# A hybrid mLSTM / gated DeltaNet layer: GpSimd's long two-operand operations cut into pieces of 256 columns

## The chip, the core and the metric

One core of one Trainium2 chip runs the whole layer. The metric is the device time in microseconds (us) of one execution. The engines are named as the profile names them: PE is the matrix engine (PEld is its weight load), DVE the vector engine, ACT the scalar engine, POOL is GpSimd, SP issues the DMAs.

## What is computed

The layer normalises x (2048 tokens of 1024 features, fp32), projects it with one matrix `w_in`, and feeds the columns to two groups of heads: four mLSTM heads (q and k of 128, v of 256) and eight gated DeltaNet heads (128 each, with a short causal convolution on q, k and v). Both are recurrences over chunks of tokens. Their gated and normalised outputs stand side by side (2048 columns), are projected with `w_out`, added to x, and normalised again. The core of the reference, cut:

```python
def step(carry, inp):                  # mLSTM, chunk by chunk
    ...
    P = jnp.exp(D - m_t[..., None]) * jnp.einsum('bhld,bhsd->bhls', qi, ki)
    num = (w_inter[..., None] * jnp.einsum('bhld,bhde->bhle', qi, C)
           + jnp.einsum('bhls,bhse->bhle', P, vi))
    ...
# gated DeltaNet, chunk by chunk: a unit lower triangular system, then a state update
sol = lax.linalg.triangular_solve(a_mat, rhs, left_side=True, lower=True, unit_diagonal=True)
U, W = sol[..., :dv], sol[..., dv:]
def step(S, inp):
    qi, ki, Ui, Wi, Ai, gi = inp
    v_new = Ui - jnp.einsum('bhld,bhde->bhle', Wi, S)
    o = (jnp.einsum('bhld,bhde->bhle', qi * jnp.exp(gi)[..., None], S)
         + jnp.einsum('bhls,bhse->bhle', Ai, v_new))
    ...
```

## The kernel before

**Layout.** The tokens are done in 4 segments of 512, each of 4 chunks of 128. A segment runs 8 windows in turn, P0 M0 P1 M1 P2 M2 P3 M3: P windows are pairs of DeltaNet heads, M windows mLSTM heads (the last segment has P3 before M2). In a window PE multiplies the segment's normalised input with the window's columns of `w_in`, and between these matmuls the chunk work of earlier windows is woven in. After the last segment comes the tail: 16 tiles of 128 tokens, each transposed and multiplied with `w_out`.

**Products in two parts.** Every fp32 product of the projections is made of three matmuls on parts: each operand is split into a high part (a cast, `hi`) and a low part (the operand less its high part, `lo`), and hi·hi, hi·lo and lo·hi are added in one PSUM tile. So each split needs a cast on ACT and a subtraction with two SBUF operands on DVE or POOL. Input parts are `hh` and `hl`, weight parts `whi` and `wlo`.

**Weights.** In segment 0 `split_w` loads a raw half (`wraw`, 128 x 1024), ACT casts it in two pieces of 512 columns (L175), and one subtraction makes the low part (L177): on DVE for the first four weights, on POOL for the 58 halves after them. Both parts are also written to DRAM (L181), and segments 1 to 3 load them from there (L157) with no splitting. The names ending in _P belong to P windows, those in _M to M windows. PE reads a weight half as four steps k of 256 columns: L343 to L345 for the projections that keep features on the partitions (`pf_...`), L355 to L357 for those that keep tokens there (`pt_...`); L345 and L356 are the ones that read `wlo`.

**Other two-operand work of POOL.** `load_h` scales the next segment's input by the row norm (`rbc`, L316) and the gain (`attn_c`, L319), 8 halves of 512 columns a segment, for segments 1 to 3. Once per DeltaNet head q (`gq`) is multiplied by its decay `gbc` (L845), 512 columns; the mLSTM multiplies `qw` by `qT` (L541) and splits it (L553). In the tail POOL applies the gain to the transposed tile (`ytt`, L1188) and makes its low part (`ylo`, L1153), four groups of 512 columns for each token tile.

**Work around it on DVE.** The solver of the triangular blocks is 31 pairs of a product `tb` (L816) and a subtraction `xb` (L820), both on SBUF alone. Others read one operand from PSUM (`gyt`, L985: the gate on the product `op`), or move 32 x 32 blocks (stream transposes: L484, and L1185 for the tail).

**Order.** PE's order is the order of the code. That of the other engines' queues is set when the kernel is built, by a scheduler that simulates the instructions; each engine then runs its own queue strictly in turn and waits on semaphores. A semaphore wait covers the part of a tile that was written, not the whole tile: who reads one piece waits for the instruction that wrote this piece.

Of the kernel before, what the change touches and what calls it, by code (L numbers as in the profile page):

```python
# [10 lines left out]
F32 = mybir.dt.float32  # L11
F32R = mybir.dt.float32r
AF = mybir.ActivationFunctionType
ALU = mybir.AluOpType
# [3 lines left out]
P = 128  # L18
D = 1024
KT = D // P  # L20
T = 512
# [24 lines left out]
RAW = 'hkhrhrkkkrrry'  # L46
WOM = 2
WFP = 100
GN = 4


VT = ((0, 1, 1, 1), (1, 1, 1, 1), (1, 0, 0, 0))
# [13 lines left out]
def hybrid_layer(  # L66
# [16 lines left out]
    nc = tc.nc  # L83
# [34 lines left out]
    attn_c = cst.tile([P, KT], F32, name="attn_c")  # L118
# [29 lines left out]
    def unit(ncol, dt, nm):  # L148
        return wp.tile([P, HK, ncol], dt, tag="wu", name=nm, bufs=10)
# [11 lines left out]
    def split_w(key, src, ncol, nm, between):  # L161

        raws = [unit(ncol, F32, f"wraw_{nm}_{i}") for i in range(2)]
        step = 2 if between else HK
        for k in range(0, KT, step):
            nc.sync.dma_start(raws[k // HK][:, k % HK:k % HK + step, :], src[:, k:k + step, :])
            if between:
                between()
        his, los = ([unit(ncol, F32R, f"{p_}_{nm}_{i}") for i in range(2)] for p_ in ("whi", "wlo"))
        eng = nc.vector if len(wloads) > nloads - WDV else nc.gpsimd  # L170
        for k in range(0, KT, step):
            i, k0 = k // HK, k % HK
            hi, lo, raw_ = his[i], los[i], raws[i]
            for q in range(k0, k0 + step, 2):
                nc.scalar.copy(hi[:, q:q + 2, :], raw_[:, q:q + 2, :])  # L175
            ks = slice(k0, k0 + step)
            eng.tensor_tensor(lo[:, ks, :], raw_[:, ks, :], hi[:, ks, :].bitcast(F32), op=ALU.subtract)  # L177
        kept = parts_d[key] = ypool.tile([2, 2, P, HK, ncol], F32, tag=f"wd{nm}", name=f"wd{nm}")
        for i in range(2):
            for part, t_ in enumerate((his[i], los[i])):  # L180
                nc.sync.dma_start(kept[part, i], t_.bitcast(F32))  # L181
        return his, los
# [121 lines left out]
    def load_h(seg, rbc):  # L304
        xks = []
        for t in range(NCH):
            if t == 2:
                ab = [sm.tile([P, 4, P], F32, tag="xin", name=f"xk{seg}_{t}_{i}") for i in range(2)]
            else:
                pool, tag, bufs = (wkp, "lbt", 1) if t == 3 else (sm, "xk", XKB)  # L310
                xk = pool.tile([P, KT, P], F32, tag=tag, name=f"xk{seg}_{t}", bufs=bufs)
                ab = [xk[:, 0:4, :], xk[:, 4:8, :]]
            c0 = seg * T + t * P
            for i in range(2):
                nc.sync.dma_start(ab[i], xT[:, i * 4:(i + 1) * 4, c0:c0 + P])
                nc.gpsimd.tensor_tensor(  # L316
                    ab[i], ab[i], rbc[:, t * P:(t + 1) * P].unsqueeze(1).broadcast_to([P, 4, P]),
                    op=ALU.mult)
                nc.gpsimd.tensor_tensor(  # L319
                    ab[i], ab[i], attn_c[:, i * 4:(i + 1) * 4].unsqueeze(2).broadcast_to([P, 4, P]),  # L320
                    op=ALU.mult)
            xks.append(ab)
        return xks

# [151 lines left out]
    def by_dve(which, seg, pr):  # L476
        return which[2 if seg == NSEG - 1 else min(seg, 1)][pr]
# [49 lines left out]
    def m_chunks(seg, h, r, st):  # L527
        s_ = f"{seg}_{h}"
        qT, kT, vt, G = r["q"], r["k"], r["v"], r["g"]
# [8 lines left out]
                pt[:, cs], nm[:, cs], ccol[:, c, h:h + 1], negmask, op0=ALU.add, op1=ALU.min)  # L538
            nc.scalar.activation(nm[:, cs], nm[:, cs], AF.Exp, bias=mprev[:, c, h:h + 1])
        qw = nm  # L540
        nc.gpsimd.tensor_tensor(qw, qw, qT, op=ALU.mult)  # L541
        nc.scalar.activation(pt, pt, AF.Exp)
        kq = psc.tile([P, 512], F32, tag="cp", name=f"kq{s_}")
        for c in range(NCH):
# [4 lines left out]
        if fast:  # L549
            def split(a, nm, pool, tag, eng, **kw):  # L550
                t_ = pool.tile([P, 2, T], F32R, tag=tag, name=f"{nm}{s_}", **kw)
                nc.scalar.copy(t_[:, 0, :], a)
                eng.tensor_tensor(t_[:, 1, :], a, t_[:, 0, :].bitcast(F32), op=ALU.subtract)  # L553
                return t_
            ps2 = split(pt, "pts", wkp, "lbt", nc.vector)
            qw2 = split(qw, "qws", sm, "xk", nc.gpsimd, bufs=XKB)
# [146 lines left out]
    def g_prep(seg, pr, r, st):  # L703
        s_ = f"{seg}_{pr}"
        h0 = pr * 2
        qT, kT = [r["q", 0], r["q", 1]], [r["k", 0], r["k", 1]]
# [3 lines left out]
        ua, gbcs = [uat[:, 0], uat[:, 1]], []  # L710
# [103 lines left out]
        for i in range(31):  # L814
            n = 31 - i
# [14 lines left out]
        for j in range(2):  # L830
            tp = psc.tile([P, 512], F32, tag="cp", name=f"qtp{s_}_{j}")
            if by_dve(QT, seg, pr):
                nc.scalar.activation(tp, qT[j], AF.Square)
                nc.vector.tensor_reduce(qs[:, j], tp.rearrange("p (b i) -> p b i", i=32),
                                        axis=mybir.AxisListType.X, op=ALU.add,
                                        apply_transpose=True)
            else:
                for c in range(NCH):
                    nc.tensor.transpose(tp[:, c * P:(c + 1) * P], qT[j][:, c * P:(c + 1) * P], ident)
                for c in range(NCH):  # L840
                    cs = slice(c * P, (c + 1) * P)
                    nc.scalar.activation(tp[:, cs], tp[:, cs], AF.Square,
                                         accum_out=ssq[:, c, j:j + 1])
            nc.scalar.activation(gbcs[j], gbcs[j], AF.Exp)
            nc.gpsimd.tensor_tensor(qT[j], qT[j], gbcs[j], op=ALU.mult)  # L845
            yield
        if by_dve(QT, seg, pr):

# [219 lines left out]
    for seg in range(NSEG):  # L1068
# [17 lines left out]
        for kind, n in ORDER_LAST if last else ORDER:  # L1086
            r = {}
            streams, keep = [], ()
            if kind == "P":
                q = 3 if n == 0 else n - 1  # L1090
# [54 lines left out]
    def gains(k, n):  # L1145
        return gain_c[:, k:k + n].unsqueeze(2).broadcast_to([P, n, P])

    def y_split(t, k4, yt_, eng, res):

        yh = fa.tile([P, 4, P], F32R, tag=f"yh{k4}", name=f"yh{t}_{k4}")  # L1150
        ylo = fa.tile([P, 4, P], F32R, tag=f"ylo{k4}", name=f"ylo{t}_{k4}")
        nc.scalar.copy(yh, yt_)  # L1152
        eng.tensor_tensor(ylo, yt_, yh.bitcast(F32), op=ALU.subtract)  # L1153
        res[k4] = yh, ylo

    def y_pe(t, yl, res):
# [18 lines left out]
    def y_dve(t, yl):  # L1175

        yts, n = [], 16 // len(yl)
        for k in range(0, 16, n):
# [4 lines left out]
            for a in range(4):  # L1183
                for b in range(4):
                    nc.vector.transpose(ytt[32 * b:32 * b + 32, :, 32 * a:32 * a + 32],  # L1185
                                        y3[32 * a:32 * a + 32, :, 32 * b:32 * b + 32])
            for c in range(0, n, GN):
                nc.gpsimd.tensor_tensor(ytt[:, c:c + GN, :], ytt[:, c:c + GN, :],  # L1188
                                        gains(k + c, GN), op=ALU.mult)
            yts += [ytt[:, c:c + 4, :] for c in range(0, n, 4)]  # L1190
# [78 lines left out]
    def raw_rows(k):  # L1269
        c = RAW[k - 3]  # L1270
        if c == "h":
            return raw_halves(k)
        if c == "k":
            return [sm.tile([P, D], F32, tag="xk", name=f"wor{k}", bufs=XKB)]
        if c == "r":
            return [fa.tile([P, D], F32, tag="xr", name=f"wor{k}", bufs=2)]
        return [fc.tile([P, D], F32, tag="yl", name=f"wor{k}", bufs=2)]

    for k in range(3, 16):
# [3 lines left out]
        raw_ = raw_rows(k)  # L1283
# [86 lines left out]
```

## Time and profile before

| | |
|---|---|
| three runs | 2354.9, 2358.06, 2360.65 us; median 2358.06 |
| the profiled execution | 2354.22 us; its span (first to last instruction) is 2352.2 us |
| mean granted TensorE clock in it | 0.976 of full speed |
| PE busy | 2225.8 us (95%) |
| DVE busy | 1925.3 us (82%) |
| ACT busy | 876.1 us (37%) |
| POOL busy | 714.5 us (30%), 820 instructions |

Busy time is the time in which an engine executes an instruction. An instruction of DVE or POOL that is held out of SBUF by another engine counts as busy for as long as it is held, so a busy engine is not always a working one: the same operation at two different durations is the sign to look for.

### The profile page before, as it was taken

To read this page: it belongs to the slowest core of one execution; us is meant where nothing else is said; L and a number is where in the kernel's file an instruction comes from. 1 tells how busy PE (TensorE), PEld (TensorE's weight loads), DVE (VectorE), ACT (ScalarE), POOL (GpSimd) and SP (SyncE) were. 2 spreads that over 40 slices of the span, in tenths; PEclk is the share of its full clock that TensorE was granted. 3 is DMA by queue.
4 is the path that set the end of the run, shared out by engine and by line. 5 is a ranking of instruction groups with operands and counts; after the bars stand their busy time and mean duration, and the time that the engine had idled before them with its cause. 6 is when DMAs were issued, how large, how long until landed. Compare 5 with 4: busy or idle time off the path is not lost.

```text
span 2352.2 us, 41574 instructions
## 1 busy us (share of the span) xinstructions
PE 2225.8 (95%) x14750; PEld 1970.7 (84%) x14750; DVE 1925.3 (82%) x5359; ACT 876.1 (37%) x2351; POOL 714.5 (30%) x820
## 2 busy tenths in 40 slices
PE   8889899889899999998999999999999999999998
PEld 7778788788789898887898989888988997777777
DVE  7989898996988888879888888788766837988784
ACT  5535454544333434343333343443334234111111
POOL 4435353451302121413020214130212114444433
PEclk9889999999999999999999999999999999999999
DMA  7766657574445554645454556454546455222221
GB/s 254 249 204 233 233 188 245 184 267 156 163 155 182 171 194 168 223 155 174 155 182 158 191 176 232 146 182 157 183 169 205 166 194 159 73 99 90 99 81 63
DMA packets 183320, 409.18 MB, mean 174 GB/s; under 512 B 51736, under 2 KB 84632, under 8 KB 183112
## 3 DMA queue, kind: packets, MB, share of 16 engines
q1 hardware_dynamic: 182392, 405.74, 50.9%
q8 instruction: 116, 1.90, 0.3%
q14 instruction: 92, 0.75, 0.1%
q10 hardware_dynamic: 720, 0.79, 0.1%
HBM read 309.68 MB, written 96.90 MB: 173 GB/s over the span
## 4 chain that ended last, share of the span: by engine, by line
PE 45%; DVE 37%; DMA 6%; issue 5%; ACT 3%; POOL 3%; SPq 0%; POOLq 0%; ACTq 0%; DVEq 0%
DVE ytt L1185 6%; DVE ktok L484 3%; DVE tb L816 3%; DVE xb L820 3%; DVE gv L484 2%; DVE kw L484 2%; PE pt_mz L355 2%; PE pt_mz L356 2%; PE pt_mz L357 2%; PE pt_mo L355 2%; PE pt_mo L356 2%; PE pt_mo L357 2%; PE pt_gz L356 2%; PE pt_gz L355 2%; PE pt_gz L357 2%
## 5 line engine op out<-in xcount | busy, mean ns | idle before, releaser
L1185 DVE STREAM_TRANSPOSE ytt<-yl 32x256 f32<-32x256 f32 x448 | 195.1, 436 | 42.0 <-POOL ylo L1153 35.9
L816 DVE TENSOR_TENSOR tb<-xb,lbt 128x248 f32<-128x248 f32 (+30 forms) x496 | 181.2, 365 | 20.5 <-DMA lbt<-l_d 7.7
L820 DVE TENSOR_TENSOR xb<-xb,tb 128x248 f32<-128x248 f32 (+30 forms) x496 | 172.0, 347 | 12.7
L983 POOL TENSOR_TENSOR gms<-gms,nhalf 128x2 f32<-128x2 f32 x64 | 46.8, 730 | 421.9 <-DVE gms L981 421.5
L355 PE MATMUL pt_mv<-whi_M,hh 128*128 128x256 f32 x512 | 149.3, 292 | 12.4 <-DVE vlo L511 8.3
L355 PE MATMUL pt_gz<-whi_P,hh 128*128 128x256 f32 (+1 forms) x512 | 153.8, 300 | 2.8 <-ACT whi_P L175 1.7
L355 PE MATMUL pt_mz<-whi_M,hh 128*128 128x256 f32 x512 | 150.1, 293 | 5.6 <-DVE tz L522 4.8
L355 PE MATMUL pt_mo<-whi_M,hh 128*128 128x256 f32 x512 | 149.4, 292 | 4.3 <-DVE vlo L511 4.3
L357 PE MATMUL pt_gz<-whi_P,hl 128*128 128x256 f32 (+1 forms) x512 | 148.3, 290 | 1.5 <-DVE mr L630 1.5
L356 PE MATMUL pt_gz<-wlo_P,hh 128*128 128x256 f32 (+1 forms) x512 | 148.4, 290 | 1.4 <-DVE wlo_P L177 1.4
L356 PE MATMUL pt_mv<-wlo_M,hh 128*128 128x256 f32 x512 | 145.9, 285 | 0.0
L357 PE MATMUL pt_mv<-whi_M,hl 128*128 128x256 f32 x512 | 145.8, 285 | 0.0
L357 PE MATMUL pt_mz<-whi_M,hl 128*128 128x256 f32 x512 | 145.8, 285 | 0.0
L356 PE MATMUL pt_mz<-wlo_M,hh 128*128 128x256 f32 x512 | 145.8, 285 | 0.0
L357 PE MATMUL pt_mo<-whi_M,hl 128*128 128x256 f32 x512 | 144.7, 283 | 0.0
L356 PE MATMUL pt_mo<-wlo_M,hh 128*128 128x256 f32 x512 | 144.6, 282 | 0.0
L1233 ACT ACTIVATE jkf<-xr 128x512 f32<-128x512 f32 (+1 forms) x33 | 20.5, 620 | 278.5 <-DVE xr L1231 144.9
L484 DVE STREAM_TRANSPOSE ktok<-gk 32x128 f32<-32x128 f32 x384 | 116.1, 302 | 5.4
L484 DVE STREAM_TRANSPOSE gv<-xingv 32x128 f32<-32x128 f32 x384 | 116.0, 302 | 5.4
L1226 PE MATMUL po<-woh,ylo 128*128 128x512 f32 (+1 forms) x297 | 115.1, 388 | 0.6 <-POOL ylo L1153 0.6
L1224 PE MATMUL po<-woh,yh 128*128 128x512 f32 (+1 forms) x297 | 114.5, 386 | 0.9 <-ACT yh L1152 0.9
L1225 PE MATMUL po<-wol,yh 128*128 128x512 f32 (+1 forms) x297 | 114.7, 386 | 0.2 <-POOL wol L1032 0.2
(403 smaller groups left out, 7535.9 us busy)
## 6 DMA issues: line engine op xcount, KB each, us to landing
whi_M<-wdM SPq DMA_DIRECT2D x96, 512.0 KB, 3.9
wlo_M<-wdM SPq DMA_DIRECT2D x96, 512.0 KB, 5.3
whi_P<-wdP SPq DMA_DIRECT2D x90, 512.0 KB, 3.8
wlo_P<-wdP SPq DMA_DIRECT2D x90, 512.0 KB, 5.0
wraw_M<-in_wg_dram SPq DMA_DIRECT2D x32, 512.0 KB, 6.8
wdM<-whi_M SPq DMA_DIRECT2D x32, 512.0 KB, 3.0
wdM<-wlo_M SPq DMA_DIRECT2D x32, 512.0 KB, 5.7
wraw_P<-in_wg_dram SPq DMA_DIRECT2D x30, 512.0 KB, 6.0
```

The costliest lines, as they stand in the source:

```text
L355: nc.tensor.matmul(ps, lhsT=hh[k][:, ts], rhs=hi, start=(k == 0), stop=False)
L356: nc.tensor.matmul(ps, lhsT=hh[k][:, ts], rhs=lo, start=False, stop=False)
L357: nc.tensor.matmul(ps, lhsT=hl[k][:, ts], rhs=hi, start=False, stop=(k == KT - 1))
L484: nc.vector.transpose(dst[32 * a:32 * a + 32, :, 32 * b:32 * b + 32], s4[32 * b:32 * b + 32, :, a, :])
L816: nc.vector.tensor_tensor(tb[:, :, 0:n], xb[:, :, i:i + 1].broadcast_to([P, 8, n]), lbt[:, i:i + 1, i + 1:32].broadcast_to([P, 8, n]), op= ...
L820: nc.vector.tensor_tensor(xs, xs, tb[:, :, 0:n], op=ALU.subtract)
L983: nc.gpsimd.tensor_tensor(ms, ms, nhalf[:, 0:2], op=ALU.pow)
L1185: nc.vector.transpose(ytt[32 * b:32 * b + 32, :, 32 * a:32 * a + 32], y3[32 * a:32 * a + 32, :, 32 * b:32 * b + 32])
L1224: nc.tensor.matmul(ps, lhsT=yh, rhs=woh, start=(k == 0), stop=False)
L1225: nc.tensor.matmul(ps, lhsT=yh, rhs=wol, start=False, stop=False)
L1226: nc.tensor.matmul(ps, lhsT=ylo, rhs=woh, start=False, stop=(k == 15))
L1233: nc.scalar.activation(jk[:, 0:n], xr[:, cs], AF.Square, accum_out=ssf[:, i:i + 1])
```

## The change

POOL's subtractions and products with two operands of 512 or 1024 columns are issued as several instructions of 256 columns each, over the same data in the same tiles. The work per element is the same, and so are the variants of the same lines that run on DVE. POOL's instructions go from 820 to 1146.

```diff
-GN = 4
+GN = 2
...
-            eng.tensor_tensor(lo[:, ks, :], raw_[:, ks, :], hi[:, ks, :].bitcast(F32), op=ALU.subtract)
+            for ks in [ks] if eng is nc.vector else [slice(q, q + 1) for q in range(k0, k0 + step)]:
+                eng.tensor_tensor(
+                    lo[:, ks, :], raw_[:, ks, :], hi[:, ks, :].bitcast(F32), op=ALU.subtract)
...
-                nc.gpsimd.tensor_tensor(
-                    ab[i], ab[i], rbc[:, t * P:(t + 1) * P].unsqueeze(1).broadcast_to([P, 4, P]),
-                    op=ALU.mult)
-                nc.gpsimd.tensor_tensor(
-                    ab[i], ab[i], attn_c[:, i * 4:(i + 1) * 4].unsqueeze(2).broadcast_to([P, 4, P]),
-                    op=ALU.mult)
+                for k in range(0, 4, 2):
+                    a_ = ab[i][:, k:k + 2]
+                    nc.gpsimd.tensor_tensor(
+                        a_, a_, rbc[:, t * P:(t + 1) * P].unsqueeze(1).broadcast_to([P, 2, P]),
+                        op=ALU.mult)
+                    nc.gpsimd.tensor_tensor(
+                        a_, a_, attn_c[:, i * 4 + k:i * 4 + k + 2].unsqueeze(2).broadcast_to([P, 2, P]),
+                        op=ALU.mult)
...
-        nc.gpsimd.tensor_tensor(qw, qw, qT, op=ALU.mult)
+        for hs in (slice(0, T // 2), slice(T // 2, T)):
+            nc.gpsimd.tensor_tensor(qw[:, hs], qw[:, hs], qT[:, hs], op=ALU.mult)
...
-                eng.tensor_tensor(t_[:, 1, :], a, t_[:, 0, :].bitcast(F32), op=ALU.subtract)
+                n = T if eng is nc.vector else T // 2
+                for i in range(0, T, n):
+                    hs = slice(i, i + n)
+                    eng.tensor_tensor(
+                        t_[:, 1, hs], a[:, hs], t_[:, 0, hs].bitcast(F32), op=ALU.subtract)
...
-            nc.gpsimd.tensor_tensor(qT[j], qT[j], gbcs[j], op=ALU.mult)
+            for hs in (slice(0, T // 2), slice(T // 2, T)):
+                nc.gpsimd.tensor_tensor(qT[j][:, hs], qT[j][:, hs], gbcs[j][:, hs], op=ALU.mult)
...
-        eng.tensor_tensor(ylo, yt_, yh.bitcast(F32), op=ALU.subtract)
+        for ks in [slice(0, 4)] if eng is nc.vector else [slice(0, 2), slice(2, 4)]:
+            eng.tensor_tensor(ylo[:, ks], yt_[:, ks], yh[:, ks].bitcast(F32), op=ALU.subtract)
```

`GN` is the number of 128-column blocks that one gain operation of L1188 takes. Cut are, on POOL: L177 (58 operations, each now four), and in two pieces each L316 and L319 (24 each), L541 (16), L553 (10), L845 (32), L1153 (60) and L1188 (60).

The first place is POOL's queue early in segment 0, at the first weight whose low part POOL makes (`wlo_P_0_2`, the DeltaNet pair 0, third weight, in two halves); `halo` and `xingq` are the convolution's borders. Before:

```order
L177 TENSOR_TENSOR wlo_P_0_2_0_565<-wraw_P_0_2_0_559,whi_P_0_2_0_563 128x1024 [waits DMAHW1_49,DMAHW7_49,PE_49,Activation_49]
L663 COPY halo<-xingq_0_0_605 128x3 [waits Activation_49,Pool_49]
L661 COPY xingq_0_1_642<-halo 128x3 [waits DVE_49]
L177 TENSOR_TENSOR wlo_P_0_2_1_566<-wraw_P_0_2_1_560,whi_P_0_2_1_564 128x1024 [waits DMAHW2_49,DMAHW3_49,DMAHW0_49,Activation_49]
L663 COPY halo<-xingq_0_1_642 128x3 [waits Activation_49,Pool_49]
```

After (the fourth piece, which has no wait as the second, is left out at the dots):

```order
L178 TENSOR_TENSOR wlo_P_0_2_0_565<-wraw_P_0_2_0_559,whi_P_0_2_0_563 128x256 [waits DMAHW1_49,DMAHW7_49,PE_49,Activation_49]
L178 TENSOR_TENSOR wlo_P_0_2_0_565<-wraw_P_0_2_0_559,whi_P_0_2_0_563 128x256
L178 TENSOR_TENSOR wlo_P_0_2_0_565<-wraw_P_0_2_0_559,whi_P_0_2_0_563 128x256 [waits Activation_49]
...
L672 COPY halo<-xingq_0_0_611 128x3 [waits Activation_49,Pool_49]
L670 COPY xingq_0_1_648<-halo 128x3 [waits DVE_49]
L178 TENSOR_TENSOR wlo_P_0_2_1_566<-wraw_P_0_2_1_560,whi_P_0_2_1_564 128x256 [waits DMAHW2_49,DMAHW3_49,DMAHW0_49,Activation_49]
```

One instruction became four in the same place. The first and the third wait for ACT, since each of ACT's two casts covers two pieces; the halo copies stand behind all four as they stood behind the one.

The second place is PE's queue in the tail: the first k steps of a token tile's product `po`, with the tile's high and low parts `yh` and `ylo` and the parts of `w_out` (named by the buffers that they live in). Before:

```order
L1224 MATMUL po_0_24529<-wua_22637,yh_0_24424 128x512 [waits DVE_49,Activation_49]
L1225 MATMUL po_0_24529<-wua_22637,yh_0_24424 128x512
L1226 MATMUL po_0_24529<-wua_22637,ylo_0_24425 128x512 [waits Pool_49]
L1224 MATMUL po_0_24529<-wE_22755,yh_0_24424 128x512
L1225 MATMUL po_0_24529<-wgg_22756,yh_0_24424 128x512
L1226 MATMUL po_0_24529<-wE_22755,ylo_0_24425 128x512
L1224 MATMUL po_0_24529<-wgk_22912,yh_0_24424 128x512
L1225 MATMUL po_0_24529<-wgq_22914,yh_0_24424 128x512
L1226 MATMUL po_0_24529<-wgk_22912,ylo_0_24425 128x512
```

After:

```order
L1235 MATMUL po_0_24861<-wua_22916,yh_0_24748 128x512 [waits DVE_49,Activation_49]
L1236 MATMUL po_0_24861<-wua_22916,yh_0_24748 128x512
L1237 MATMUL po_0_24861<-wua_22916,ylo_0_24749 128x512 [waits Pool_49]
L1235 MATMUL po_0_24861<-wE_23034,yh_0_24748 128x512
L1236 MATMUL po_0_24861<-wgg_23035,yh_0_24748 128x512
L1237 MATMUL po_0_24861<-wE_23034,ylo_0_24749 128x512
L1235 MATMUL po_0_24861<-wgk_23191,yh_0_24748 128x512
L1236 MATMUL po_0_24861<-wgq_23193,yh_0_24748 128x512
L1237 MATMUL po_0_24861<-wgk_23191,ylo_0_24749 128x512 [waits Pool_49]
```

The rows and their order are the same; the wait for POOL that stood at the first k alone covers one of two pieces now, and the third k has a wait for the other.

The third place is SP's queue in segment 1, between the DeltaNet pairs 2 and 3 (`gbc_3_0` and `gbc_3_1` load pair 3's decays, `l_d` and `lbt` are pair 2's way to its solver through DRAM, `nm` belongs to an mLSTM head, L157 loads weights); at the dots three more `l_d` are left out. Before:

```order
L716 DMA gbc_3_0_11042<-rows_6441 128x512 [waits DMAHW5_49,Pool_49]
L716 DMA gbc_3_1_11049<-rows_6441 128x512 [waits DMAHW6_49,Pool_49]
L533 DMA nm_2_10374<-rows_6441 128x512 [waits DMAHW7_49,PE_49]
L157 DMA whi_M_2_2_1_9881<-wdM_2_2_4024 128x1024 [waits DMAHW0_49,PE_49]
L807 DMA l_d_2_9693<-ua_2_9626 32x8x32 [waits DMAHW1_49,DVE_49]
...
L988 DMA yd_73<-gyt_1_1_9749 128x256 [waits DMAHW5_49,DVE_49]
L157 DMA wlo_M_2_2_1_9883<-wdM_2_2_4024 128x1024 [waits DMAHW6_49,PE_49]
L157 DMA whi_M_2_3_0_10014<-wdM_2_3_4173 128x1024 [waits DMAHW7_49,PE_49]
L157 DMA wlo_M_2_3_0_10016<-wdM_2_3_4173 128x1024 [waits DMAHW0_49,PE_49]
L811 DMA lbt_2_9772<-l_d_2_9693 32x1024 [waits DMAHW3_49,DMAHW2_49,DMAHW4_49,DMAHW1_49,Activation_49]
```

After:

```order
L725 DMA gbc_3_0_11259<-rows_6646 128x512 [waits DMAHW5_49,Activation_49,Pool_49]
L537 DMA nm_2_10589<-rows_6646 128x512 [waits DMAHW6_49,PE_49]
L157 DMA whi_M_2_2_1_10096<-wdM_2_2_4154 128x1024 [waits DMAHW7_49,PE_49]
L157 DMA wlo_M_2_2_1_10098<-wdM_2_2_4154 128x1024 [waits DMAHW0_49,PE_49]
L816 DMA l_d_2_9906<-ua_2_9839 32x8x32 [waits DMAHW1_49,DVE_49]
...
L998 DMA yd_73<-gyt_1_1_9962 128x256 [waits DMAHW5_49,DVE_49]
L157 DMA whi_M_2_3_0_10229<-wdM_2_3_4309 128x1024 [waits DMAHW6_49,PE_49]
L157 DMA wlo_M_2_3_0_10231<-wdM_2_3_4309 128x1024 [waits DMAHW7_49,PE_49]
L725 DMA gbc_3_1_11266<-rows_6646 128x512 [waits DMAHW0_49,Activation_49,Pool_49]
L820 DMA lbt_2_9985<-l_d_2_9906 32x1024 [waits DMAHW3_49,DMAHW2_49,DMAHW4_49,DMAHW1_49,Activation_49]
```

The second decay load, which waits for POOL, moved from ahead of `l_d` and four weight loads to behind them, right ahead of `lbt`; a low weight part moved ahead of `l_d`.

## Rows read from the trace of the kernel before

**Rows 1.** The page: busy time by engine, and the chain that ended last.
```profile
PE 2225.8 (95%) x14750; PEld 1970.7 (84%) x14750; DVE 1925.3 (82%) x5359; ACT 876.1 (37%) x2351; POOL 714.5 (30%) x820
...
PE 45%; DVE 37%; DMA 6%; issue 5%; ACT 3%; POOL 3%; SPq 0%; POOLq 0%; ACTq 0%; DVEq 0%
```

**Rows 2.** Windows: stretch, length, busy PE, PEld, DVE, ACT, POOL; clock, DMA share, GB/s.
```profile
45.00:630.00 585.00, 519.45 (x3450) 462.50 (x3448) 520.18 (x1331) 279.35 (x719) 249.62 (x224) 0.94 0.63 214
630.00:975.00 345.00, 339.06 (x2470) 308.51 (x2471) 294.94 (x935) 130.65 (x374) 60.55 (x101) 0.99 0.52 178
975.00:1030.00 55.00, 50.44 (x370) 47.88 (x369) 45.60 (x133) 13.44 (x41) 24.71 (x27) 0.97 0.54 176
1450.00:1500.00 50.00, 44.32 (x336) 41.84 (x334) 42.57 (x118) 12.62 (x38) 22.68 (x23) 1.00 0.54 178
1960.00:2352.00 392.00, 371.15 (x1647) 298.95 (x1646) 307.08 (x656) 74.79 (x168) 176.70 (x156) 0.98 0.30 97
```

**Rows 3.** PE's waits, 45 to 630 us: sum, times, longest.
```profile
PE sp L940 <- DVE SS L971: 11.3, 4, 3.8
PE fp L884 <- ACT dmz L879: 7.6, 2, 4.2
...
PE pf_gv L345 <- POOL wlo_P L177: 1.2, 2, 1.1
```

**Rows 4.** Timelines of DVE, then POOL, around 500 us: start, us, operation.
```profile
500.40 2.43 DVE L816 TENSOR_TENSOR tb<-xb,lbt 128x200 f32<-128x200 f32 x1
502.87 1.34 DVE L820 TENSOR_TENSOR xb<-xb,tb 128x200 f32<-128x200 f32 x1
...
510.75 0.34 DVE L816 TENSOR_TENSOR tb<-xb,lbt 128x176 f32<-128x176 f32 x1
...
500.15 2.46 POOL L177 TENSOR_TENSOR wlo_M<-wraw_M,whi_M 128x1024 fp32r<-128x1024 f32 x1 [3.07 <-ACT whi_M L175]
502.56 1.43 POOL L316 TENSOR_TENSOR xk<-xk,rbc 128x512 f32<-128x512 f32 x1
```

**Rows 5.** Timelines of DVE, then POOL, around 483 us.
```profile
483.14 0.59 DVE L985 SCALAR_TENSOR_TENSOR gyt<-op,gms,gg 128x128 f32<-128x128 f32 x2
...
483.29 2.40 POOL L177 TENSOR_TENSOR wlo_M<-wraw_M,whi_M 128x1024 fp32r<-128x1024 f32 x1 [0.56 <-ACT whi_M L175]
```

**Rows 6.** Lines: shortest/median/longest ns, first and last start.
```profile
L177 POOL TENSOR_TENSOR wlo_M<-wraw_M,whi_M x32: 2347/2406/2638, 66.2 to 504.0; 128x1024 fp32r<-128x1024 f32 x32
...
L845 POOL TENSOR_TENSOR gq<-gq,gbc x32: 1266/1291/1580, 88.2 to 1844.3; 128x512 f32<-128x512 f32 x32
...
L770 DVE TENSOR_TENSOR kl<-gk,kh x28: 404/418/426, 198.6 to 1730.3; 128x256 fp32r<-128x256 f32 x28
```

**Rows 7.** Timelines of POOL, then DVE, around 324 us: pieces of 256 columns.
```profile
322.82 0.75 POOL L770 TENSOR_TENSOR kl_pt<-gq,kh 128x256 fp32r<-128x256 f32 x1
323.51 0.78 POOL L770 TENSOR_TENSOR kl_nm<-gq,kh 128x256 fp32r<-128x256 f32 x1
324.21 1.64 POOL L770 TENSOR_TENSOR kl<-gq,kh 128x256 fp32r<-128x256 f32 x2
...
324.43 0.83 DVE L770 TENSOR_TENSOR kl_pt<-gk,kh 128x256 fp32r<-128x256 f32 x1
```

**Rows 8.** The tail: DVE line, timelines of POOL and DVE, a PE wait.
```profile
L1247 DVE SCALAR_TENSOR_TENSOR xr<-xr,sc,fn_bc x30: 748/1525/1553, 2024.7 to 2328.6; 128x512 f32<-128x512 f32 x30
...
2157.40 2.49 POOL L1188 TENSOR_TENSOR ytt<-ytt,gain_c 128x512 f32<-128x512 f32 x2
2162.43 5.08 POOL L1153 TENSOR_TENSOR ylo<-ytt,yh 128x512 fp32r<-128x512 f32 x4 [2.54 <-ACT yh L1152]
...
2165.01 5.37 DVE L1185 STREAM_TRANSPOSE ytt<-yl 32x256 f32<-32x256 f32 x12 [2.98 <-POOL ylo L1153]
...
PE po L1226 <- POOL ylo L1153: 7.6, 13, 0.7
```

**Rows 9.** SP's waits for a step: sum, times, longest.
```profile
SPq L716 <- POOL gq L845: 66.0, 17, 13.3
```

## The prediction

> **What bounds the kernel now.** I read the page first. PE is busy 95% of the span and DVE 82%, and the chain that ended last runs over PE for 45% of the span, over DVE for 37% and over POOL for 3% [rows 1]. POOL, the only engine whose instructions are cut, is busy 30%. So the change can pay only through DVE and PE, and I looked for where POOL's work makes these two wait.
>
> Then the windows, for the place. From 45 to 630 us, almost all of segment 0, PE is idle 585 - 519.45 = 65.5 us and its granted clock is 0.94; DVE is busy 520.18 of the 585 us, 89%. From 630 to 975 us PE is idle 6 of 345 us at 0.99. Two short stretches at the ends of segments 1 and 2 have idle shares like those of segment 0 (4.6 of 55 us, 5.7 of 50), and the tail from 1960 us on has 20.9 us idle [rows 2]. The early stretch is where POOL makes the low weight parts, 249.62 us of work there.
>
> Then PE's waits in the early stretch: they end at DVE and ACT, mostly in the chunk chains (`sp`, `fp`: 11.3 and 7.6 us), and only 1.2 us at POOL itself [rows 3]. So POOL's long operations can matter there through DVE. The timelines show how. In the solver, where a pair `tb`, `xb` takes 0.34 us each, a `tb` that starts 0.25 us after a POOL subtraction of 1024 columns lasts 2.43 us and ends 0.2 us after it, and an `xb` that meets a POOL product of 512 columns lasts 1.34 us [rows 4]. A DVE operation with one operand in PSUM runs beside the same subtraction untouched: two `gyt` in 0.59 us [rows 5]. So a DVE operation with both operands in SBUF is held for as long as POOL's runs, and the two alternate one for one. I went through the timelines of both engines operation by operation: 35 of the 58 L177 on POOL hold a DVE operation by over 1.2 us beyond its duration elsewhere, 69 us in all (the first of [rows 4], 2.43 for 0.34, is one of them).
>
> **Costs, part by part.**
>
> *Price of a piece.* L177 takes 2406 ns for 1024 columns, L845 1291 ns for 512 [rows 6]. POOL operations of 256 columns start 0.69 us apart, and a DVE operation of 256 columns takes 0.83 us beside one, where its twins take 0.418: it is held 0.41 us [rows 7]. So POOL pays 4 x 0.69 - 2.41 = 0.35 us more for each of 58 L177, and 2 x 0.69 - 1.29 = 0.09 us for each of 226 operations of 512 columns: 20 + 20 = 40 us. It is spread over a POOL that is idle 1637 us, which hides it; without that cover all 40 would be paid. I take 0.
>
> *Low weight parts (58), on DVE's time.* A held operation loses 2.09 us now (2.43 - 0.34). With pieces it waits for the piece under way, 0.41 us, and goes next. What follows decides. If DVE's next operations also have two SBUF operands, each of the four pieces holds one of them: 4 x 0.41 = 1.64, and up to 2.1 where a piece holds half a microsecond; the gain is 0 to 0.45 us. If a transpose or an operation from PSUM follows, it runs beside the rest and about two pieces hold something: 2.09 - 0.82 = 1.27 us gained. Of the 35 I count about half of either kind (solver and conv chains on one side, chunk work between transposes and PSUM on the other): 17 x 1.27 = 21.6 us, and nothing for the others. DVE is 89% busy there, so about a ninth only lengthens its own idle time: **-19 us**. Bounds: 0 (all alternate) and 35 x 1.27 x 0.89 = -40.
>
> The Trainium skill (SBUF — State Buffer, "Who interferes with whom") says that a DVE instruction with two SBUF inputs contends with a GpSimd instruction that reads SBUF, that the holder keeps the shared ports for its whole instruction and that the other side blocks fully. The 2.43 us beside 0.34 agree. Read strictly the rule speaks against the change: the columns that POOL must read are as many as before, and a queue of nothing but such operations gains nothing. It is the first rival below.
>
> *PE's clock.* At 0.94 the stretch has the work of 35 us at full clock less than it could have. Were that loss to fall with PE's idle time, 20 of 65.5 us, it would return 10.7 us. Many idle stretches have other causes (`fp` waits for ACT), so I take a quarter to a third: **-3 us**, bounds 0 and -11.
>
> *PE's own waits for low parts.* PE now waits for the first of four pieces and not for the whole [rows 3]; at 0.69 instead of 2.41 us the 1.2 us go: **-1 us**, bounds 0 and -1.2.
>
> *The input scaling (L316, L319), three stretches.* The two later ones have 4.6 + 5.7 = 10.3 us idle in 105; at the rate of 630 to 975 us (6 in 345) 1.8 were normal, so 8.5 us are in question [rows 2]. A product of 512 columns holds 1.0 us (1.34 - 0.34), two pieces hold 0.82 if both hold something and 0.41 if one: a gain of 0.2 to 0.6 of it. I take a third: **-3 us**, bounds 0 and -8.5.
>
> *The tail.* PE waits for the first `ylo` of a tile 7.6 us in 13 waits, 0.58 us each [rows 8]. The first of two pieces comes 1.27 - 0.69 = 0.58 us sooner, so the wait as such goes. But the tile's pace is DVE's too: it waits 2.98 us for `ylo` before the next transposes, and before that its two L1247, 0.75 us each alone, take 2.99 us beside two gains of POOL. After, the last gain piece ends nearer to them, some 0.5 us sooner (two times a wait of about 0.41 + the rest of a turn), while two `ylo` of 2.54 us become four pieces of 2.76, +0.22. That makes -0.3 us for each of 13 tiles: **-4 us**, bounds +3 (0.22 x 13, no gain at L1247) and -7.6.
>
> *Queues.* In SP's queue the second decay load goes behind `l_d` and the weights. It waits for POOL's `gq`; such waits held up SP 66.0 us in 17 times, once 13.3 [rows 9]. What stood behind it (weights, `l_d`) goes sooner; behind it stays `lbt`, which starts the solver and itself waits for `l_d` to land. I take 0; if `gq` came after that landing, the solver would start later by the difference.
>
> Sum: -19 - 3 - 1 - 3 - 4 = **-30 us**. The profiled execution took 2354.2 us, 2.0 more than its span, so 2324; the median of the runs lies 3.8 us above it, so **2328 us**.
>
> **Rivals.**
>
> *A. The hold is only shared out.* DVE's queue in segment 0 is dense with two-operand operations, every piece holds one, and the four together as much as the one did. For it: the solver runs 31 pairs in a row, and [rows 4] show the strict turn-taking. Against: half of the 35 stand among transposes or PSUM operations as in [rows 5]. Left are PE's own waits, the tail and a little of the scaling: -1 - 4 - 3 = -8, so 2350 us.
>
> *B. POOL's own work comes late (slower).* Turn-taking works both ways: a DVE operation can go between two pieces, so a low part in the solver takes 4 x 0.69 + 4 x 0.35 = 4.2 us and not 2.4. What is behind it in POOL's queue, the small powers for the norms of the chunk chains above all, comes 1.8 us later, and the chains are what PE waits for. If a third of the 58 delays land on the chain, it is 58 / 3 x 1.8 = 35, against the 30 of the sum: +5; with half, +22, so about 2371 us in the middle. It decides once more than some 17 of 58 reach the path (30 / 1.8). Against it: PE waited for POOL only 1.2 us there on the row shown, and POOL is idle more than half of the stretch.
>
> *C. The clock and the chunk chains answer in full.* The chains of segment 0 feed each other, so an early result shortens several waits: half of PE's idle time (33 us), half of the clock's loss (17), the whole wait of the tail (7.6) and 5 us of the scaling: -63, 2295 us. For it: 69 us of held time against 65.5 us of idle time. Against: ACT ends some of those waits.
>
> **How the numbers follow.** Forecast 0.57 (its own range 2310 to 2344), A 0.22 (2344 to 2357), B 0.13 (2357 to 2385), C 0.08 (2285 to 2310). Runs of this kernel tell apart about 0.2%, 4.7 us. The range 2303 to 2358 leaves out nearly all of B and most of C, 0.18. Faster: forecast, C and two thirds of A, 0.79; same: the rest of A and the near end of B, 0.10; slower: 0.11.
>
> **What the profile after would show.** If right: 45 to 630 us shortens by some 20 us, its DVE busy time falls from 520 by about as much, PE's clock there rises to 0.95 or more; no solver `tb` lasts over 1.2 us; `sp` waits are fewer; L1247 has a median near 1.2 us; the tail's `ylo` wait is near 0.2 us a tile or gone; POOL's busy time rises by 40 to 55 us. If A: DVE's busy time is as before, with many operations at 0.75 to 0.9 us in place of few at 2.4. If B: POOL-ended waits of the chains grow. What would make it wrong: the two halves of the 35 counted badly, since the answer hangs on what DVE does next; or the scheduler's new order of segment 0 on ACT, DVE and SP, which I have priced at nothing.

## The result and the profile after

The changed kernel takes 2319.64 us (median of four runs, 2316.57 to 2321.76), the kernel before 2356.48 us beside it (2353.8 to 2360.65): a ratio of 0.9841, 95% interval 0.9821 to 0.9861. That is 36.8 us, where the forecast was 2328 and -30. The profiled execution took 2320.7 us with a span of 2318.9, which is 33.3 us less than the span of before. POOL's instructions went from 820 to 1220, as the page shows, and not to 1146 as said ahead of the prediction: 58 x 3 + 226 = 400 more.

The page of the changed kernel, its busy times and the chain that ended last:

```profile
PE 2212.4 (95%) x14750; PEld 1964.7 (85%) x14750; DVE 1888.6 (81%) x5359; ACT 875.5 (38%) x2351; POOL 800.4 (35%) x1220
...
PE 56%; DVE 30%; DMA 7%; ACT 3%; issue 2%; POOL 1%; SPq 1%; ACTq 0%; POOLq 0%; DVEq 0%
```

Beside [rows 1], POOL is busy 86 us more and DVE 37 us less, and the chain runs over PE for 56% and over DVE for 30%, where it was 45% and 37%. The windows of the changed kernel, cut, to within ten matmuls, where the work of [rows 2] begins and ends:

```profile
45.00:607.00 562.00, 509.68 (x3452) 455.80 (x3450) 499.82 (x1332) 280.68 (x720) 297.76 (x432) 0.96 0.65 223
607.00:952.00 345.00, 338.23 (x2460) 307.57 (x2459) 293.13 (x930) 128.65 (x369) 60.54 (x112) 0.99 0.51 176
952.00:1006.00 54.00, 49.71 (x378) 47.69 (x379) 44.48 (x138) 14.63 (x46) 29.54 (x44) 1.00 0.58 189
1427.00:1474.00 47.00, 43.75 (x338) 41.92 (x336) 39.52 (x119) 12.17 (x37) 25.58 (x39) 1.00 0.59 194
1935.00:2319.00 384.00, 368.07 (x1638) 298.29 (x1636) 296.14 (x655) 74.30 (x166) 199.20 (x274) 0.99 0.31 100
```

The early stretch became 23 us shorter, the tail 8, the two short scaling stretches 1 and 3; the quiet stretch of 345 us holds 2460 matmuls where it held 2470. In the early stretch DVE is busy 20 us less. PE is idle 52.3 us there (65.5 before) and busy 509.7 (519.5 before) for the same matmuls, at a granted clock of 0.96 instead of 0.94 of full speed; both are means over stretches at the two levels, 2.4 and 1.2 GHz.

The timelines of DVE and then POOL in the solver near the end of segment 0, the place of [rows 4]:

```profile
484.94 0.78 DVE L829 TENSOR_TENSOR xb<-xb,tb 128x192 f32<-128x192 f32 x1
485.75 0.77 DVE L825 TENSOR_TENSOR tb<-xb,lbt 128x184 f32<-128x184 f32 x1
486.56 0.77 DVE L829 TENSOR_TENSOR xb<-xb,tb 128x184 f32<-128x184 f32 x1
487.37 0.76 DVE L825 TENSOR_TENSOR tb<-xb,lbt 128x176 f32<-128x176 f32 x1
...
483.83 1.68 POOL L178 TENSOR_TENSOR wlo_M<-wraw_M,whi_M 128x256 fp32r<-128x256 f32 x2
485.46 0.85 POOL L320 TENSOR_TENSOR xk<-xk,rbc 128x256 f32<-128x256 f32 x1
486.28 1.66 POOL L178 TENSOR_TENSOR wlo_M<-wraw_M,whi_M 128x256 fp32r<-128x256 f32 x2
```

Here every DVE operation meets a piece. None is held for 2 us any more, but each takes 0.77 us where a free one takes 0.34, and POOL's pieces come 0.81 to 0.83 us apart where they come 0.69 apart alone: the two engines take turns. Over the whole run the longest `tb` is 0.90 us, 2.46 before. Line by line (shortest/median/longest ns):

```profile
L825 DVE TENSOR_TENSOR tb<-xb,lbt x496: 132/304/899, 103.1 to 1854.3; 128x248 f32<-128x248 f32 x6, 128x224 f32<-128x224 f32 x6, 128x200 f32<-128x200 f32 x6, 128x176 f32<-128x176 f32 x6
...
L178 POOL TENSOR_TENSOR wlo_M<-wraw_M,whi_M x128: 712/742/1261, 58.6 to 489.5; 128x256 fp32r<-128x256 f32 x128
...
L1258 DVE SCALAR_TENSOR_TENSOR xr<-xr,sc,fn_bc x30: 746/1098/1175, 1999.0 to 2296.4; 128x512 f32<-128x512 f32 x30
```

And PE's waits in the early stretch (45 to 607 us):

```profile
PE pt_mv L359 <- DVE vlo L515: 9.3, 3, 5.3
PE sp L950 <- DVE SS L981: 9.0, 4, 2.6
PE fp L894 <- ACT dmz L889: 6.7, 3, 3.5
...
PE pf_gv L349 <- POOL wlo_P L178: 1.7, 3, 1.2
```

The chain waits are a little smaller (`sp` 11.3 to 9.0 us, `fp` 7.6 to 6.7); the wait for low parts did not shrink, it is 1.7 us in three where it was 1.2 in two [rows 3]. In the tail PE's wait for POOL's `ylo` is gone: from 1935 us on no such row is left.

### The profile page after: what moved, and what is told of

Read it like the earlier page. It is cut to its first block, busy times and chain, and to the rows that moved or that the text cites. A ratio compares the mean times of both kernels' runs of the same rounds, so it can differ in the third digit from the quotient of the medians.

```text
span 2318.9 us, 41978 instructions
## 1 busy us (share of the span) xinstructions
PE 2212.4 (95%) x14750; PEld 1964.7 (85%) x14750; DVE 1888.6 (81%) x5359; ACT 875.5 (38%) x2351; POOL 800.4 (35%) x1220
## 4 chain that ended last, share of the span: by engine, by line
PE 56%; DVE 30%; DMA 7%; ACT 3%; issue 2%; POOL 1%; SPq 1%; ACTq 0%; POOLq 0%; DVEq 0%
PE po L1237 5%; PE po L1236 5%; PE po L1235 5%; DVE ktok L488 3%; DVE xb L829 3%; DVE tb L825 3%; DVE kw L488 2%; DVE gv L488 2%; PE pt_mo L359 2%; PE pt_mo L360 2%; PE pt_mo L361 2%; PE pt_gz L361 2%; PE pt_mz L359 2%; PE pt_gz L360 2%; PE pt_gz L359 2%
## 5 line engine op out<-in xcount | busy, mean ns | idle before, releaser
L825 DVE TENSOR_TENSOR tb<-xb,lbt 128x248 f32<-128x248 f32 (+30 forms) x496 | 168.0, 339 | 21.0 <-DMA lbt<-l_d 8.0
L1244 ACT ACTIVATE jkf<-xr 128x512 f32<-128x512 f32 (+1 forms) x33 | 20.4, 619 | 266.9 <-DVE xr L1242 143.5
```

Of the source, the lines that this page charges most:

```text
L825: nc.vector.tensor_tensor(tb[:, :, 0:n], xb[:, :, i:i + 1].broadcast_to([P, 8, n]), lbt[:, i:i + 1, i + 1:32].broadcast_to([P, 8, n]), op= ...
L1244: nc.scalar.activation(jk[:, 0:n], xr[:, cs], AF.Square, accum_out=ssf[:, i:i + 1])
```

## The experiments

Three theories had to be told apart. **Theory 1**, that of the prediction: DVE is held for one piece and not for the whole operation. **Theory 2**: the scheduler, given other instructions, puts the queues in another order, and this order is faster. **Theory 3**: PE and the DMAs start on the first piece of a tile.

### Where the gain is: one part alone, and all but that part

```diff
 # e1_wlo_only: the kernel before, with L177 alone cut; e2_all_but_wlo: the change, with L177 whole
...
+            for ks in [ks] if eng is nc.vector else [slice(q, q + 1) for q in range(k0, k0 + step)]:
+                eng.tensor_tensor(
+                    lo[:, ks, :], raw_[:, ks, :], hi[:, ks, :].bitcast(F32), op=ALU.subtract)
```

> Only the low weight parts (L177) are cut into four pieces; all else is as before. Theory 1 (DVE is held for a piece of 0.4 us and not for 2 us): segment 0 gets its 23 us, and the tail and the two later scaling stretches get nothing: about 2333 us where the kernel before takes 2356, ratio 0.990. Theory 2 (the gain belongs to the queues' new order, or to all cuts together): a smaller part of the 37 us, under 12, ratio above 0.995.

> All cuts but that of the low weight parts, which stay whole. Theory 1: segment 0 as before; the scaling stretches give 3 to 5 us and the tail 7: about 2345 us, ratio 0.9955. Theory 2: the rest of what the low parts alone don't give, 20 us or more, ratio under 0.992. The two runs together should add up to the whole change (0.984) by theory 1.

The low weight parts alone give 2331.14 us, ratio 0.9898 (0.988 to 0.9916); all the rest gives 2341.34, ratio 0.9934 (0.9919 to 0.9948). 25 and 15 us add up to 40, against 37 for the whole change, which is within the intervals: the parts act apart from each other, as theory 1 has it, and the low weight parts are two thirds of it. The second run fits neither of its expectations (0.9955, and under 0.992). Its trace gives 7 us in the tail, as expected, and 6 us from 630 us to the tail where 3 to 5 were expected.

### Is it the order of the queues?

```diff
 # p1_cut_old_order: all cuts; p2_whole_new_order: none. Every queue is chained in a given order
...
+        for s in steps:
+            at += s + 1
+            if last is not None:
+                tc.add_manual_dep(own[at], last, mybir.DependencyInfo(
+                    mybir.DependencyClass.NoSync, mybir.DependencyReason.DATA), reason="pin")
+            last = own[at].name
```

An edge of this kind sets only the order of issue, with no wait. With it DVE, ACT, SP and POOL of the cut kernel were put in exactly the order of the kernel before, and the other way round; PE's order is the same in both anyway.

> All cuts of the change, but every queue (DVE, ACT, SP, POOL) is pinned to the order of the kernel before, the pieces standing where the whole operation stood. Theory 1 (shorter holds): nearly all of the gain is kept, 2318 to 2325 us, ratio 0.984 to 0.987. Theory 2 (the scheduler's new order is a large part of the gain, as the uneven pieces, 24 us faster with the long hold kept, suggest): 2328 to 2340 us, ratio 0.988 to 0.993.

> No cut at all, but every queue is pinned to the order of the changed kernel, a whole operation standing where its first piece stands. Theory 1: no gain, 2352 to 2360 us, ratio 0.998 to 1.002. Theory 2: a third to a half of the 37 us, 2338 to 2345 us, ratio 0.992 to 0.995.

The cut kernel in the old order takes 2319.26 us, ratio 0.9838 (0.9823 to 0.9852), the same as the change. The whole operations in the new order take 2356.55, ratio 1.0004 (0.9993 to 1.0015). So the cuts make the gain, and the order, the moved decay load included, makes no difference beyond 0.15%. Theory 2 falls.

### Is it the first piece that others start on?

```diff
 # e4_wlo_reversed: the change, pieces from the last to the first
-            for ks in [ks] if eng is nc.vector else [slice(q, q + 1) for q in range(k0, k0 + step)]:
+            for ks in [ks] if eng is nc.vector else [slice(q, q + 1) for q in reversed(range(k0, k0 + step))]:
```

> All of the change, but the four pieces of a low weight part are made from the last to the first, so PE's first step has to wait for all four. Theory 1: PE's earlier start on a first piece is worth 1 to 2 us, DVE's shorter holds are as in the change: 2320 to 2323 us, ratio 0.985. Theory 3 (the gain of segment 0 is PE and the DMAs starting on single pieces): most of the 23 us of segment 0 are lost, about 2340 us, ratio 0.993.

2319.34 us, ratio 0.9841 (0.9825 to 0.9858): nothing is lost, though PE's first step now has to wait for the piece that is made last. Theory 3 falls, and with it the prediction's -1 us for PE's own waits.

### As many instructions, but a long one among them

```diff
 # e7_wlo_uneven (order left to the scheduler), p3_uneven_new_order (pinned to the order of the change)
...
+            for cs in [slice(0, ncol)] if eng is nc.vector else [
+                    slice(0, 232), slice(232, 240), slice(240, 248), slice(248, 256)]:
+                eng.tensor_tensor(
+                    lo[:, ks, cs], raw_[:, ks, cs], hi[:, ks, cs].bitcast(F32), op=ALU.subtract)
```

> All of the change, but the four pieces of a low weight part are one of 928 columns and three of 32. As many instructions as in the change, but the long hold of DVE is back. Theory 1: nearly all of segment 0's gain is lost (a hold of 2.1 to 2.2 us, and POOL pays some 0.2 us more for each small piece): 2342 to 2350 us, ratio 0.995. Theory 2 (number of instructions, new order in the queues): the gain stays, about 2320 us, ratio 0.985.

> The uneven pieces of the low weight parts (928 and three of 32 columns), with every queue pinned to the order of the changed kernel: against the change only the length of the holds differs. Theory 1: segment 0 loses its gain, 2338 to 2345 us, ratio 0.993 to 0.995. Theory 2: 2320 to 2330 us, ratio 0.985 to 0.989.

2332.40 us (0.9894, 0.9877 to 0.9912) and 2332.49 (0.9894, 0.9877 to 0.991). Both lie between the two expectations: 13 us of the gain are lost, and about 9 are kept against the whole operation in `e2_all_but_wlo`. I had taken the three small pieces for a mere cost. The timelines of the pinned kernel, DVE then POOL, show that they are gaps:

```profile
496.83 2.22 DVE L830 TENSOR_TENSOR xb<-xb,tb 128x200 f32<-128x200 f32 x1
499.09 0.36 DVE L826 TENSOR_TENSOR tb<-xb,lbt 128x192 f32<-128x192 f32 x1
499.48 0.36 DVE L830 TENSOR_TENSOR xb<-xb,tb 128x192 f32<-128x192 f32 x1
499.87 0.35 DVE L826 TENSOR_TENSOR tb<-xb,lbt 128x184 f32<-128x184 f32 x1
...
496.61 3.34 POOL L179 TENSOR_TENSOR wlo_M<-wraw_M,whi_M 128x928 fp32r<-128x928 f32 x4 [3.51 <-ACT whi_M L175]
```

The 928 columns hold an `xb` to 2.22 us, and then two solver operations go through at their free length while POOL spends its time on pieces of 32 columns. In the kernel before the next long POOL operation took that turn [rows 4]. So a part of the hold had gone in these kernels too, which the table below shows, and the two runs did not put the whole hold back as they were meant to.

### Other lengths, and no reading at all

```diff
 # e5_wlo_512: the change with two pieces; e6_wlo_128: with eight
-            for ks in [ks] if eng is nc.vector else [slice(q, q + 1) for q in range(k0, k0 + step)]:
+            for ks in [ks] if eng is nc.vector else [slice(q, q + 2) for q in range(k0, k0 + step, 2)]:
...
+            for ks, cs in [(ks, slice(0, ncol))] if eng is nc.vector else [
+                    (slice(q, q + 1), slice(c, c + 128)) for q in range(k0, k0 + step) for c in (0, 128)]:
...
 # e10_no_read: the change and its order, with zeros in place of the low parts that POOL makes
+                if eng is nc.gpsimd:
+                    nc.gpsimd.memset(lo[:, ks, :].bitcast(F32), 0.0)
+                    continue
```

> All of the change, but the low weight parts are cut into two pieces of 512 columns and not four of 256. A held DVE operation waits about 1 us for the piece under way and not 0.41. Theory 1: between whole (2341) and four pieces (2320), 2329 to 2334 us, ratio 0.988 to 0.990. If one early end were all that counts (PE's first piece, one gap for DVE): 2320 to 2324.

> All of the change, but the low weight parts are cut into eight pieces of 128 columns. Theory 1: a hold of some 0.25 us, and DVE gets between more pieces; less is left to gain, and POOL pays about 0.5 us more for a low part (0.135 us for each further instruction): 2312 to 2318 us, ratio 0.981 to 0.984. If POOL's own time begins to count (29 us more in segment 0): 2320 to 2328, ratio 0.985 to 0.988.

> All of the change and its queue orders, but POOL fills the low weight parts with zeros, in the same pieces and at the same places, and reads nothing for it: the low part of those weights is left out of the products. It shows what the holds by L177 still cost in the changed kernel (53 us of DVE time by the trace). Theory 1 with its measured rate, about 1.1 us of time for 1 us of hold in segment 0: up to 50 us less, 2268 to 2290 us, ratio 0.963 to 0.972. If something else bounds segment 0 by now: above 2305 us, ratio over 0.978.

Two pieces give 2326.40 us (0.9875, 0.9859 to 0.9892), between the two expectations of that run (2329 to 2334, and 2320 to 2324). Eight give 2312.24 (0.9803, 0.9785 to 0.9821), as theory 1 had it, and this is the fastest version that computes the layer. Zeros give 2274.50 (0.9648, 0.9633 to 0.9664). The last kernel does more than take away the hold, since a fill of 256 columns takes POOL 0.31 us and not 0.74 and waits for no cast, so it bounds what the holds still cost and does not measure it.

The windows of `e10_no_read`, the line of POOL in it, and a place in its solver (DVE, then POOL):

```profile
45.00:560.00 515.00, 490.73 (x3447) 440.54 (x3445) 446.86 (x1327) 277.91 (x716) 175.05 (x427) 0.99 0.70 242
...
L179 POOL MEMSET wlo_M<- x128: 301/311/484, 52.6 to 444.9; 128x256 f32 x128
...
94.62 0.40 DVE L828 TENSOR_TENSOR tb<-xb,lbt 128x232 f32<-128x232 f32 x1
95.06 0.40 DVE L832 TENSOR_TENSOR xb<-xb,tb 128x232 f32<-128x232 f32 x1
...
94.61 1.07 POOL L179 MEMSET wlo_M<- 128x256 f32 x4 [0.57 <-PE pt_mv L364]
```

The line of POOL in `e6_wlo_128`, and PE's waits for it from 45 to 592 us:

```profile
L179 POOL TENSOR_TENSOR wlo_M<-wraw_M,whi_M x256: 442/462/1006, 60.6 to 480.0; 128x128 fp32r<-128x128 f32 x128
...
PE pt_mv L361 <- POOL wlo_M L179: 5.1, 4, 2.6
PE pf_gv L350 <- POOL wlo_P L179: 1.8, 2, 1.4
```

With eight pieces PE waits 6.9 us for low parts where it waited 1.7 with four, so POOL's own time begins to count there. With zeros the early work takes about 515 us for 585, PE is idle 24 us of them, and the clock is at 0.99.

For a table I added up, for segment 0 from the same PE matmul to the same PE matmul, how much longer DVE's operations that overlap a POOL operation are than the same operations without overlap (each kernel's own profiled execution):

| kernel | L177 in | DVE held, us | length, us |
|---|---|---|---|
| before | 1 piece | 94.9 | 586.5 |
| p2, whole in the new order | 1 | 95.5 | 587.1 |
| e2, all but L177 | 1 | 90.8 | 586.9 |
| e7 / p3, uneven | 928 + 3 x 32 | 83.7 / 81.3 | 571.9 / 577.8 |
| e5 | 2 | 80.2 | 566.3 |
| the change | 4 | 73.4 | 563.7 |
| p1, cut in the old order | 4 | 71.2 | 563.3 |
| e6 | 8 | 52.0 | 547.8 |
| e10, zeros | none reads | 16.1 | 516.2 |

A straight line through these and the other kernels' values has a slope of 0.93 us of time for 1 us of hold and leaves no kernel more than 6.5 us off. Three things limit it. How the duration without overlap is taken moves single sums by 3 to 4 us, though not their order. `e8` and `e9` (under "The tail"), with segment 0 as before, have lengths of 592.0 and 589.9 us, so a length alone can be 5 us off. And the profiled execution of `e6` was the fastest of its four, 6.8 us below their median, while that of `p3` was the slowest, 6.8 above: by the medians, eight pieces gain 7.4 us on four for 21.4 us less of hold, a third of the slope. L177 holds DVE 74 us as one piece, 66 as two, 54 as four and 33 as eight.

### The tail

```diff
 # e8_gains_only: the kernel before with
-GN = 4
+GN = 2
 # e9_ylo_only: the kernel before with
-        eng.tensor_tensor(ylo, yt_, yh.bitcast(F32), op=ALU.subtract)
+        for ks in [slice(0, 4)] if eng is nc.vector else [slice(0, 2), slice(2, 4)]:
+            eng.tensor_tensor(ylo[:, ks], yt_[:, ks], yh[:, ks].bitcast(F32), op=ALU.subtract)
```

> Only the gains of the tail (L1188) are cut in two. The tail's loop runs through DVE: transposes, the two L1247 held by the gains, the sum, the norm, the cast, the low part, transposes. The pair of L1247 loses 0.85 us of its 2.99, which is more than the 0.59 us that PE waits in a tile: PE's wait goes, 0.59 x 13 = 7.7 us: 2348 to 2350 us, ratio 0.9965 to 0.997. If both cuts of the tail were needed: under 3 us, ratio over 0.9985.

> Only L1153 in the tail is cut in two. By the prediction's working of the tail, PE's wait of 0.58 us a tile for the first low part goes, but DVE's transposes come 0.22 us later: -3 to +3 us, 2353 to 2359, ratio 0.9987 to 1.0013. The other reading (the tail's 7.5 us come from PE's shorter wait): 2349 us, ratio 0.997.

The gains alone give 2348.64 us, ratio 0.9961 (0.9949 to 0.9973). The low parts `ylo` alone give 2359.55, ratio 1.001 (1.0 to 1.0019): at best nothing, rather a loss of 2 us. PE's waits of a stretch of the tail (2000 to 2300 us) in `e9_ylo_only` tell why:

```profile
PE po L1225 <- ACT yh L1152: 9.6, 13, 1.9
```

The wait for `ylo` (6.4 us in 11 waits in this stretch before) is gone, but PE now waits more often and longer for the high part `yh`, one step earlier in the loop. The loop is DVE's: transposes, the two L1247, the sum, ACT's norm and cast, the low part, the next transposes. The timeline of DVE in the changed kernel shows one turn of it:

```profile
2128.01 0.44 DVE L1196 STREAM_TRANSPOSE ytt<-yl 32x256 f32<-32x256 f32 x1
2128.64 2.14 DVE L1258 SCALAR_TENSOR_TENSOR xr<-xr,sc,fn_bc 128x512 f32<-128x512 f32 x2 [0.18 <-POOL sc L1254]
2130.70 0.67 DVE L1242 TENSOR_TENSOR xr<-xr,po 128x512 f32<-128x512 f32 x1
2132.21 0.15 DVE L1247 TENSOR_SCALAR sc<-ssf 128x1 f32<-128x1 f32 x1 [0.84 <-ACT jkf L1244]
2135.64 7.18 DVE L1196 STREAM_TRANSPOSE ytt<-yl 32x256 f32<-32x256 f32 x16 [3.28 <-POOL ylo L1164]
...
2150.41 0.44 DVE L1196 STREAM_TRANSPOSE ytt<-yl 32x256 f32<-32x256 f32 x1
```

The pair (L1258 now) takes 2.14 us for 2.99, the wait for `ylo` 3.28 for 2.98 [rows 8], and a turn 22.40 us (2150.41 - 2128.01). The same lines with `ylo` alone cut:

```profile
2161.98 0.44 DVE L1186 STREAM_TRANSPOSE ytt<-yl 32x256 f32<-32x256 f32 x1
2162.60 3.00 DVE L1248 SCALAR_TENSOR_TENSOR xr<-xr,sc,fn_bc 128x512 f32<-128x512 f32 x2 [0.18 <-POOL sc L1244]
...
2170.46 7.19 DVE L1186 STREAM_TRANSPOSE ytt<-yl 32x256 f32<-32x256 f32 x16 [3.27 <-POOL ylo L1154]
...
2185.23 0.44 DVE L1186 STREAM_TRANSPOSE ytt<-yl 32x256 f32<-32x256 f32 x1
```

The pair stays at 3.00, the wait is 3.27, and a turn takes 23.25 us, where it took 22.94 before. So the shorter gains pay 0.85 us a turn and the pieces of `ylo` cost 0.3 of it. With the gains alone nearly every turn takes 22.12 us, and the 96 matmuls of a tile, when PE never waits, start over after 22.11: there DVE is no longer the slower one. From the first matmul after 1960 us in the kernel before to the end, the tail takes 392.2 us before, 396.8 with `ylo` alone, 382.7 with the gains alone and 385.0 in the change. The change would thus be some 2 us faster with `ylo` whole; no run has that together with the other cuts.

## Why the prediction was right

**The mechanism** was right and is shown: only the cuts matter (`p1`, `p2`), they matter by the length of the hold (the table, and the uneven pieces beside as many even ones), and not by early starts (`e4`). One part of it was put too narrowly: not only operations with both operands in SBUF are held. Right behind the two `gyt` of [rows 5] stand four copies of 32 x 8 elements, and the first of them lasts to the end of POOL's operation, 2.04 us. Over the run of the kernel before, this copy and a product with one factor for each partition range like this (shortest/median/longest ns):

```profile
483.66 2.57 DVE L852 COPY ssq<-qs 32x8 f32<-32x8 f32 x4
...
L852 DVE COPY ssq<-qs x60: 148/162/2067, 94.9 to 1846.7; 32x8 f32<-32x8 f32 x60
...
L924 DVE TENSOR_SCALAR ktok<-ktok,ksc x128: 274/281/1334, 86.2 to 1840.1; 128x128 f32<-128x128 f32 x128
```

**Low weight parts, -19 us.** The early stretch lost 23 us for -19 - 3 - 1 = -23 forecast. Between fixed matmuls L177's hold fell from 74.0 to 53.6 us, 20.4 for the 21.6 worked out, and DVE's busy time fell by 20.2 for 19. That the sum came out so near is in part luck. Added up for one low part after the other in the two traces, 34 of the 58 hold a DVE operation by over 1.2 us in the kernel before. The 16 of them in the solver, taken at 0, gain 7 us together (33.4 us of hold become 26.2): four operations are held 4 x 0.43 = 1.7 us where one was held 2.09. The 18 others, set at 1.27 us each, gain 0.73, 13 us together (33.7 become 20.5), since more of the operations that follow there are held by the next pieces than was thought. So the halves were counted about right, one was sized too low and the other too high, and the two errors cancel.

**The clock, -3, and PE's own waits, -1.** Here the division was off. Between fixed matmuls PE's idle time fell by 12.8 us and its busy time by 10.0, so the clock gave 10 (matmuls are at 0.96 of full speed and not at 0.94), near the bound of 11, and the idle time less than the 20 that I gave it. The prediction counted DVE's time back as PE's idle time, while part of it came as matmuls at full clock. PE's own wait did not go, it rose by 0.5 us.

**Scaling stretches, -3.** The two later ones gave 2.7 and 4.8 us between fixed matmuls; 4 to 5 us were lost again in other windows of the profiled execution, so that the work from 607 us to the tail gave about 3 net. With the old order pinned the same work gave some 7. The difference lies in single profiled executions, and the medians (2319.26 and 2319.64) show none.

**The tail, -4.** It gave 7.2 us in the trace. The price of `ylo`, 0.22 us a tile, was near (0.3); the gain at L1247 was sized 0.5 us and is 0.85. Each operation of the pair is held by one piece, and only for 0.35 us (1.10 for 0.75); I had reckoned with 0.41 and the rest of a turn. With 0.85 - 0.3 = 0.55 us, the 13 tiles give 7.2.

**Costs taken as 0.** POOL's extra time was forecast as 40 to 55 us and is 86, since its pieces too are held by DVE (0.82 us apart in the solver). It is still hidden: PE's waits for low parts rose by 0.5 us. SP's changed queue cost nothing that shows (`p2`).

**Rivals.** A said that the pieces together hold as much as the whole. In the solver that is nearly so (1.7 for 2.09), but over segment 0 L177's sum fell by 28% with four pieces and by 56% with eight. The Trainium skill's statement on the shared ports (SBUF — State Buffer, "Who interferes with whom") agrees with the rows shown here. What rival A took from it, that an equal number of columns means an equal loss, does not follow: an operation of DVE that POOL doesn't hold, as the `gyt` of [rows 5], loses nothing beside a piece. The Trainium skill (SBUF — State Buffer, "Who interferes with whom") also says that a DVE instruction with two SBUF inputs does not contend with a GpSimd instruction that only writes SBUF. The `tb` and `xb` beside the fills of `e10` agree: 0.40 us for 232 columns, as without POOL beside them. B's price for a low part, 4.2 us, was too high (about 3.3 in the solver), and no wait of the chunk chains for POOL grew to a size that counts. C's -63 was out of reach for pieces of 256 columns: eight pieces give 45, and the zeros, which free POOL as well, 82.

The median moved 36.8 us and the trace 33.3. The remaining 3.5 are the place of either profiled execution among its runs: 1.1 us above the median after, 2.3 below it before.

## What to carry to other kernels

When POOL works on two SBUF operands while DVE works on SBUF alone, compare the duration of one DVE operation beside POOL's with the same operation alone: the excess, added up over a stretch in which DVE sets the pace, is what shorter POOL operations can give back, here about 0.9 us of time for each microsecond of hold over the whole range, and a third of that from four pieces to eight. Cut POOL's operations, above all where DVE has work waiting that POOL doesn't hold, pay for it only with idle POOL time, and try smaller pieces than seem reasonable. Where POOL's result itself stands in the loop, as `ylo` does, leave it whole.

## What was unexpected of the hardware

Pieces of 128 columns, 462 ns each for 742 at 256 columns, still paid: 2312 us for 2320, though POOL is busy 334 us early on instead of 298 and PE waits 6.9 us for low parts instead of 1.7. POOL's fills of 256 columns (0.31 us, reading nothing) left DVE's solver operations at their free length. A copy of 8 columns can last 2.07 us for 0.16 beside POOL. And the clock gave more than I had forecast: its mean in segment 0 was 0.94, 0.96 and 0.99 with PE idle 66, 54 and 25 us (before, the change, zeros), so that 10 of the 23 us that the change won in this stretch are matmuls that ran faster.
